# Feed-forward entry of a hybrid decoder block: weight requests, two rows normed in step, block sums by columns between products; norms of the last rows in a batch

## The chip, the cores and the metric

The kernel runs on one core of one Trainium2 chip. The metric is the device time of one execution in microseconds (us); lower is better. Times inside a profile are counted from the start of its span, the stretch from the first to the last instruction.

The engines are named as the profile names them: PE is TensorE (matrix products and transposes; PEld its weight loads), DVE is VectorE, ACT is ScalarE, POOL is GpSimd, and SP is the engine whose queue issues nearly all transfers here. Each works through its own instructions in order and waits for others by semaphores.

## What is computed

One decoder block over 1024 tokens of width 1024, in float32, preceded by 16 meta tokens:

```python
mix = mixer(rms_norm(h, pre_mix_norm), w_in, conv_a_w, conv_b_w, ..., w_out)
h = h + rms_norm(mix, post_mix_norm)
ff = swiglu(rms_norm(h, pre_ffn_norm), w_gate, w_up, w_down)
h = h + rms_norm(ff, post_ffn_norm)

def swiglu(xn, w_gate, w_up, w_down):
    a = jnp.einsum("btd,df->btf", xn, w_gate)
    u = jnp.einsum("btd,df->btf", xn, w_up)
    return jnp.einsum("btf,fd->btd", jax.nn.silu(a) * u, w_down)
```

The feed-forward width is 2816. `mixer` is one input projection, two groups of short convolutions with their gates, and one output projection.

## The kernel before

Every float32 operand of a product is split into a high part (a cast) and a low part (the rest), and `mm3` (lines 94 to 98) makes a product of three matmuls from them: high by high, high by low, low by high.

**Output projection and norms (lines 405 to 468).** The tokens are eight rows of 128, taken in groups (0,1,2), (3,4,5), (6,7). For each group the eight units of w_out are requested, split (cast on ACT, subtraction on POOL, line 88) and multiplied. `leave_psum` squares the result on ACT and multiplies it by the gain (tile jk). `post_mix` requests the row of x, computes an inverse root (`rsqrt_n`, a chain of small DVE instructions, each waiting for the one before), adds to get h and stores it. `ffn_norm` squares h on ACT, makes a second such chain and the normed row hn. `turn` transposes hn on PE and copies it to the four blocks `raw` (two halves of the features by two halves of the rows).

**Feed-forward, up (lines 523 to 677).** Both big products of the feed-forward are made in Strassen's manner: seven block products in place of eight, on sums of blocks. The block sums and splits of the token side (B11, B21, T1, T2, B22, T3, T4) are made once; those of the weight side for each of eleven pairs of feature blocks. A pair has weight units of w_gate (m = 0) and w_up (m = 1), each in two halves i. `order` lists the products (pair j, product n): (0,1), (1,1), (0,2), (1,2), then 6, 5, 7, 3, 4 of pair 0 and of pair 1, then the other pairs. Each has 24 matmuls. The loop at lines 663 to 677 issues a product, then the `leave` of the product before (PSUM to SBUF with the gates), then `a_side(s + LEAD)`, the weight operands of the product two further. In the first two steps it also turns rows 6 and 7; in the second it calls `prepare()` (lines 635 to 644), which makes all that is left of the token side.

**Feed-forward, down (lines 712 to 768).** Seven products of eleven steps each (`down`), with 12 matmuls a step. `run` makes operands two steps ahead (`sides`, `bsum`); the results of a product are left by `leave1` to `leave7` from the list `todo`, up to four a step. The last two steps of a product are issued bank by bank. `finish3` normalises and stores rows 0 to 3 during the last product (n = 4); `leave4` does it for rows 4 to 7 behind it.

**Order.** Up to line 465 a planner orders the instructions by simulated time. From `manual_schedule()` (line 466) to `order_.close()` (line 766) each engine issues its instructions in the order in which they are written; where the first of them fall among the planned ones is left to the planner. Pools give their buffers in turn: `tp` has five tiles of a row (gains, normed rows, weight units), `wp` three of each tag (`ws` for units as they come), `hp` four rows h.

Of the kernel before, what the change touches and what calls it, by code (L numbers as in the profile page):

```python
# [8 lines left out]
F32 = mybir.dt.float32  # L9
F32R = mybir.dt.float32r  # L10
I32 = mybir.dt.int32
AF = mybir.ActivationFunctionType
# [3 lines left out]
P = 128  # L16
# [33 lines left out]
def hybrid_block(ctx: ExitStack, tc: tile.TileContext, xT, x, w_in, w_out, w_gate, w_up, w_down, par, g_post, g_ffn, g_out, out):  # L50
# [377 lines left out]
    def ffn_norm(i, h):  # L428
# [5 lines left out]
        nc.vector.scalar_tensor_tensor(n, h, r2, gB["ffn"], op0=ALU.mult, op1=ALU.mult)  # L434
        return n

    def turn(i, n):
        c = slice((i % 4) * P, (i % 4 + 1) * P)
        for q in range(2):
            pt = aux.tile([P, 512], F32, tag="a", name=f"pt{i}_{q}")  # L440
            for k in range(4):
                nc.tensor.transpose(pt[:, k * P : (k + 1) * P], n[:, (4 * q + k) * P : (4 * q + k + 1) * P], ident)
            p4 = pt.rearrange("p (a b) -> p a b", a=4)
            nc.scalar.copy(raw[q, i // 4][:, :, c], p4)
            if (q, i // 4) == (0, 0):
                nc.vector.tensor_copy(B11[0][:, :, c], p4)
                nc.vector.tensor_tensor(B11[1][:, :, c], p4, B11[0][:, :, c].bitcast(F32), op=ALU.subtract)
# [4 lines left out]
    for grp in ((0, 1, 2), (3, 4, 5), (6, 7)):  # L452
# [16 lines left out]
    ya.close()  # L469
    p2.close()  # L470

    rp = ctx.enter_context(tc.tile_pool(name="rp", bufs=5, side="right", reuse_waits="tile"))
    st = ctx.enter_context(tc.tile_pool(name="st", bufs=13, reuse_waits="tile"))
    psf = None

    def bank(name):
        return (psf or ps2).tile([P, 512], F32, tag="p", name=name)
# [40 lines left out]
    class Pair:  # L523


        def __init__(self, j):
            self.j, self.w, self.pb, self.v = j, [], {}, {}
            for m, src in enumerate((w_gate, w_up)):
                u = []
                for i in range(2):  # L530
                    if (m + i) % 2:
                        t = tp.tile([P, TT], F32, tag="t", name=f"u{j}{m}{i}")[:, :D]
                    else:
                        t = wp.tile([P, D], F32, tag="ws", name=f"u{j}{m}{i}")
                    nc.sync.dma_start(t, src[i * NP + j])
                    u.append(t)
                self.w.append((u[0][:, :512], u[0][:, 512:], u[1][:, :512], u[1][:, 512:]))

        def a_side(self, n, m):
            a11, a12, a21, a22 = self.w[m]  # L540
# [91 lines left out]
    X = {1: B11}  # L632
    r11, r21, r12, r22 = raw[0, 0], raw[1, 0], raw[0, 1], raw[1, 1]

    def prepare():
        halves(sub, r11, r12, r11)
        X[5] = split_big(r11, "T1", (None, None))
        halves(sub, r11, r22, r11)
        X[6] = split_big(r11, "T2", (rp, rp))
        X[3] = split_big(r22, "B22", (rp, rp))  # L640
        halves(sub, r12, r22, r12)
        halves(sub, r21, r21, r11)
        X[7] = split_big(r12, "T3", (None, None))
        X[4] = split_big(r21, "T4", (None, rp))

    pairs = {0: Pair(0), 1: Pair(1)}
    order = [(j, n) for n in (1, 2) for j in range(2)] + [(j, n) for j in range(2) for n in (6, 5, 7, 3, 4)]
    order += [(j, n) for j in range(2, NP) for n in (1, 6, 2, 5, 7, 3, 4)]

    def a_side(s):  # L650
        if s >= len(order):
            return
        j, n = order[s]
        if n == 1 and 2 <= j + 1 < NP and j:
# [6 lines left out]
    for s in range(LEAD):  # L661
        a_side(s)
    for s, (j, n) in enumerate(order):
        if s == 2:
            pa.close()
            psf = ctx.enter_context(tc.tile_pool(name="psf", bufs=8, space=PSUM, reuse_waits="tile"))
        done = pairs[j].product(n, made.pop(s))
        if s < 2:
            turn(6 + s, late[6 + s])
            if s == 0:  # L670
                X[2] = split_big(r21, "B21", (None, None))
            else:
                prepare()
        if last:
            last()
        a_side(s + LEAD)
        last = done

# [21 lines left out]
    def scale(ti, r, parts, q):  # L700

        y, dq = parts[q], slice(q * 512, (q + 1) * 512)
        if q == 1:
# [8 lines left out]
    def down(n, an, bside, banks, begin, leave):  # L712
        for j in range(NP - 2):
            work.append([n, j, an, bside, [(banks[i], i, j, begin and j == 0, False, not begin, None) for i in range(4)]])
        work.append([n, NP - 2, an, bside, []])
        work.append([n, NP - 1, an, bside, [(banks[i], i, j, False, j == NP - 1, not begin, leave) for i in range(4) for j in (NP - 2, NP - 1)]])

    def load(s):
        if s < len(work):
# [23 lines left out]
    def run():  # L743
# [5 lines left out]
        for s, (n, _, _, _, mms) in enumerate(work):  # L749
# [154 lines left out]
```

## Time and profile before

| | us |
|---|---|
| two runs | 1107.70 and 1108.87, median 1108.28 |
| profiled execution | 1107.38 |
| its span | 1105.6 |

| engine | busy us | share of the span | instructions |
|---|---|---|---|
| PE | 1000.7 | 91% | 4643 |
| PEld | 841.7 | 76% | 4643 |
| DVE | 832.1 | 75% | 1176 |
| ACT | 405.1 | 37% | 640 |
| POOL | 362.2 | 33% | 201 |

The page gives for each engine the time that its instructions took. Their starts and lengths are in the timeline, together with the idle time just before an instruction and what ended it: `[22.37 <-ACT U L577]` reads: idle for 22.37 us until the ACT instruction that writes U, of line 577, was done. `x8` means eight instructions of a kind merged into one row. PE's clock is granted by the chip at one of two levels, 1.2 or 2.4 GHz; the profile gives the mean as a share of the higher.

### The profile page before, as it was taken

To read this page: it belongs to the slowest core of one execution; us is meant where nothing else is said; L and a number is where in the kernel's file an instruction comes from. 1 tells how busy PE (TensorE), PEld (TensorE's weight loads), DVE (VectorE), ACT (ScalarE), POOL (GpSimd) and SP (SyncE) were. 2 spreads that over 40 slices of the span, in tenths; PEclk is the share of its full clock that TensorE was granted. 3 is DMA by queue.
4 is the path that set the end of the run, shared out by engine and by line. 5 is a ranking of instruction groups with operands and counts; after the bars stand their busy time and mean duration, and the time that the engine had idled before them with its cause. 6 is when DMAs were issued, how large, how long until landed. Compare 5 with 4: busy or idle time off the path is not lost.

```text
span 1105.6 us, 12729 instructions
## 1 busy us (share of the span) xinstructions
PE 1000.7 (91%) x4643; PEld 841.7 (76%) x4643; DVE 832.1 (75%) x1176; ACT 405.1 (37%) x640; POOL 362.2 (33%) x201
## 2 busy tenths in 40 slices
PE   8999979797988651999999999999999899999974
PEld 8999978796867531888888888888888688887853
DVE  6499999999698849587667767767775565677696
ACT  7345221136445325223232323323231444443442
POOL 3579754254644300034133222413322300010242
PEclk9999989899999865999999999999999999999987
DMA  7111110112365250122430441243027953324232
GB/s 271 58 39 58 39 39 20 58 39 77 114 211 189 76 190 0 49 101 80 143 140 5 142 142 60 83 143 119 24 97 283 390 173 86 105 85 142 88 129 110
DMA packets 44271, 121.56 MB, mean 110 GB/s; under 512 B 4912, under 2 KB 5296, under 8 KB 42800
## 3 DMA queue, kind: packets, MB, share of 16 engines
q1 hardware_dynamic: 43632, 119.10, 31.0%
q10 hardware_dynamic: 576, 1.65, 0.5%
q8 instruction: 36, 0.59, 0.2%
q14 instruction: 27, 0.22, 0.1%
HBM read 92.16 MB, written 28.57 MB: 109 GB/s over the span
## 4 chain that ended last, share of the span: by engine, by line
PE 62%; DVE 26%; issue 5%; ACT 3%; DMA 2%; POOL 1%; POOLq 0%; SPq 0%; DVEq 0%; ACTq 0%
PE x L96 7%; PE x L98 7%; PE x L97 7%; DVE acc L280 6%; DVE z L280 5%; PE y L97 5%; PE y L96 5%; PE y L98 5%; PE qy L97 2%; PE qx L97 2%; PE qy L96 2%; PE qy L98 2%; PE qx L98 2%; PE qx L96 2%; DVE s_pm L118 1%
## 5 line engine op out<-in xcount | busy, mean ns | idle before, releaser
L502 ACT CAST op<-u 128x512 fp32r<-128x512 f32 x132 | 79.1, 618 | 210.3 <-DVE u L491 144.8
L491 DVE TENSOR_TENSOR op<-u,op 128x512 fp32r<-128x512 f32 x132 | 115.3, 899 | 50.9 <-ACT op L502 50.8
L491 DVE TENSOR_TENSOR op_da<-a,op_da 128x512 fp32r<-128x512 f32 x77 | 58.8, 764 | 70.2 <-ACT op_da L502 70.1
L280 DVE SCALAR_TENSOR_TENSOR acc<-g,pr,acc 128x512 f32<-128x512 f32 x146 | 99.9, 748 | 0.0
L494 POOL TENSOR_TENSOR C<-C,C 128x512 f32<-128x512 f32 x11 | 17.4, 1582 | 248.8 <-ACT op L502 129.4
L502 ACT CAST op_da<-a 128x512 fp32r<-128x512 f32 x77 | 47.7, 619 | 100.1 <-issue 49.0
L88 POOL TENSOR_TENSOR wl_o<-ws_o,wh_o 128x1024 fp32r<-128x1024 f32 x24 | 58.4, 2439 | 71.2 <-ACT wh_o L87 71.1
L97 PE MATMUL qx<-op_db,op_da 128*128 128x512 f32 x176 | 70.9, 403 | 9.3 <-DVE op_db L491 9.3
L494 POOL TENSOR_TENSOR U<-U,U 128x512 f32<-128x512 f32 x22 | 31.4, 1426 | 127.9 <-ACT U L606 87.6
L96 PE MATMUL qx<-op_db,op_da 128*128 128x512 f32 x176 | 70.4, 400 | 2.7 <-ACT op_db L502 2.7
L98 PE MATMUL qx<-op_db,op_da 128*128 128x512 f32 x176 | 70.0, 398 | 0.0
L488 DVE TENSOR_TENSOR U<-y,U 128x512 f32<-128x512 f32 x66 | 44.2, 684 | 27.3 <-PE y L98 25.4
L280 DVE SCALAR_TENSOR_TENSOR z<-g,pr,z 128x512 f32<-128x512 f32 x48 | 62.0, 1313 | 0.0
L491 DVE TENSOR_TENSOR op_db<-wd,op_db 128x512 fp32r<-128x512 f32 x77 | 59.2, 769 | 0.0
L96 PE MATMUL x<-B21h,op 128*128 128x512 f32 x88 | 35.5, 403 | 22.4 <-ACT U L577 22.4
L96 PE MATMUL x<-B11h,op 128*128 128x512 f32 x88 | 36.4, 414 | 17.1 <-ACT op L502 17.1
L97 PE MATMUL qy<-op_db,op_da 128*128 128x512 f32 x132 | 51.5, 390 | 0.4 <-DVE op_db L491 0.4
L98 PE MATMUL qy<-op_db,op_da 128*128 128x512 f32 x132 | 51.4, 390 | 0.0
L96 PE MATMUL qy<-op_db,op_da 128*128 128x512 f32 x132 | 51.4, 390 | 0.0
L502 ACT CAST op_db<-wd 128x512 fp32r<-128x512 f32 x77 | 47.5, 617 | 9.1 <-DVE wd L491 9.0
L97 PEld LDWEIGHTS qx<-op_db,op_da 128*128 128x128 f32 x176 | 34.0, 193 | 19.3 <-DVE op_db L491 12.4
L96 PE MATMUL p_in_h<-xh,wh_in_h 128*128 128x342 f32 x96 | 33.1, 344 | 14.9 <-DVE cv L378 14.9
(288 smaller groups left out, 3056.4 us busy)
## 6 DMA issues: line engine op xcount, KB each, us to landing
ws_o<-w_out_u SPq DMA_DIRECT2D x24, 512.0 KB, 3.6
u<-w_gate_u SPq DMA_DIRECT2D x22, 512.0 KB, 6.0
u<-w_up_u SPq DMA_DIRECT2D x22, 512.0 KB, 5.0
wd<-w_down_u SPq DMA_DIRECT2D x11, 1024.0 KB, 11.2
a<-gdS SPq DMA_DIRECT2D x44, 256.0 KB, 2.7
gdS<-GS SPq DMA_DIRECT2D x33, 256.0 KB, 4.8
a<-gdA SPq DMA_DIRECT2D x33, 256.0 KB, 3.6
xs<-xT SPq DMA_DIRECT2D x8, 520.0 KB, 6.9
```

The costliest lines, as they stand in the source:

```text
L88: (eng or nc.gpsimd).tensor_tensor(wl, ws, wh.bitcast(F32), op=ALU.subtract)
L96: nc.tensor.matmul(o, lh, rh, start=start, stop=False, skip_group_check=again)
L97: nc.tensor.matmul(o, lh, rl, start=False, stop=False, skip_group_check=again)
L98: nc.tensor.matmul(o, ll, rh, start=False, stop=stop, skip_group_check=again)
L118: nc.vector.scalar_tensor_tensor(s, t, k, s, op0=ALU.subtract, op1=ALU.mult)
L280: nc.vector.scalar_tensor_tensor(o if j == CB - 1 else p, s, wb(a, j), o if j == HEAD[a] else p, op0=ALU.mult, op1=ALU.add)
L488: (eng or nc.vector).tensor_tensor(o, a, b, op=ALU.add)
L491: (eng or nc.vector).tensor_tensor(o, a, b, op=ALU.subtract)
L494: (eng or nc.vector).tensor_tensor(o, a, b, op=ALU.mult)
L502: nc.scalar.copy(t[:, 0, :], src)
```

## The change

At the entry, the last two rows are no longer normed one after the other. Inside the hand-written order come first: the requests for rows 6 and 7 of x; the requests for the first halves of the weight units of pairs 0 and 1; the operands of the first product; then `norm_two`, which makes one chain for both rows where there were two, twice; then the second halves of pair 0. B21 is split next, its low part on POOL. `prepare()` is gone. What it summed is now summed by columns of one row of tokens each (`tsums`, two rows before the loop, one behind each `turn`), with T2 in a buffer of its own, and the splits of T2, T1, T3, B22 and T4 are each issued behind a product (`extra`).

In the down products two leaves are taken per step in place of four; the last product holds back three steps in place of two and makes its weight sums on POOL; rows 4 to 6 share one chain of the last norm, row 7 has its own and scales both its halves on DVE.

```diff
+    def residual_x(i):
+        h = hp.tile([P, D], F32, tag="h", name=f"h{i}")
+        nc.sync.dma_start(h, x[i * P : (i + 1) * P, :])
+        return h
+
+    def norm_two(grp, left, hs):
+        v = sm.tile([P, 16], F32, tag="s2", name="late1")
+        for q, i in enumerate(grp):
+            nc.vector.tensor_tensor(v[:, q : q + 1], left[i][1][:, 0:1], left[i][1][:, 1:2], op=ALU.add)
+        r = rsqrt_n(v[:, :2], 1.0 / D, RMS_EPS, 2, "pml")
+        v2 = sm.tile([P, 16], F32, tag="s2", name="late2")
+        n = {}
+        for q, i in enumerate(grp):
+            nc.vector.scalar_tensor_tensor(hs[i], left[i][0], r[:, q : q + 1], hs[i], op0=ALU.mult, op1=ALU.add)
+            n[i] = tp.tile([P, TT], F32, tag="t", name=f"hn{i}")[:, :D]
+            nc.scalar.activation(n[i], hs[i], AF.Square, accum_out=v2[:, q : q + 1])
+            nc.sync.dma_start(hd[i], hs[i])
+        r = rsqrt_n(v2[:, :2], 1.0 / D, RMS_EPS, 2, "pfl")
+        for q, i in enumerate(grp):
+            nc.vector.scalar_tensor_tensor(n[i], hs[i], r[:, q : q + 1], gB["ffn"], op0=ALU.mult, op1=ALU.mult)
+        return n
...
-    order_ = ExitStack()
-    order_.enter_context(tc.manual_schedule())
-    late = {i: post_mix(i, *left[i]) for i in grp}
-    late = {i: ffn_norm(i, late[i]) for i in grp}
...
-    def prepare():
-        halves(sub, r11, r12, r11)
-        X[5] = split_big(r11, "T1", (None, None))
-        halves(sub, r11, r22, r11)
-        X[6] = split_big(r11, "T2", (rp, rp))
-        X[3] = split_big(r22, "B22", (rp, rp))
-        halves(sub, r12, r22, r12)
-        halves(sub, r21, r21, r11)
-        X[7] = split_big(r12, "T3", (None, None))
-        X[4] = split_big(r21, "T4", (None, rp))
+    def tsums(i):
+        c = slice(i * P, (i + 1) * P)
+        sub(r11[:, :, c], r12[:, :, c], r11[:, :, c])
+        sub(T2r[:, :, c], r22[:, :, c], r11[:, :, c])
...
+    order_ = ExitStack()
+    order_.enter_context(tc.manual_schedule())
+    late_h = {i: residual_x(i) for i in grp}
+    pairs = {0: Pair(0), 1: Pair(1)}
+    pairs[0].load(0)
+    pairs[1].load(0)
+    a_side(0)
+    late = norm_two(grp, left, late_h)
+    pairs[0].load(1)
...
+    X[2] = pair("B21", (None, None))
+    copy_hi(X[2], r21)
+    for h in range(2):
+        sub(X[2][1][:, 2 * h : 2 * h + 2, :], r21[:, 2 * h : 2 * h + 2, :], X[2][0][:, 2 * h : 2 * h + 2, :].bitcast(F32), nc.gpsimd)
+    T2r = blocks(big("T2r", F32))
+    a_side(1)
+    tsums(0)
+    tsums(1)
...
+    extra = {1: t2, 2: t1, 3: t3, 4: b22, 5: t4}
     for s, (j, n) in enumerate(order):
...
         done = pairs[j].product(n, made.pop(s))
         if s < 2:
-            turn(6 + s, late[6 + s])
-            if s == 0:
-                X[2] = split_big(r21, "B21", (None, None))
-            else:
-                prepare()
+            turn(6 + s, late.pop(6 + s))
+            tsums(2 + s)
         if last:
             last()
+        if s == 2:
+            pairs[1].load(1)
+        if s in extra:
+            extra[s]()
         a_side(s + LEAD)
         last = done
...
-                for f in todo[:4]:
+                for f in todo[:2]:
                     f()
-                todo = todo[4:] + after
+                todo = todo[2:] + after
...
-        mul(t, t, g0, nc.gpsimd if i < 2 else nc.vector)
-        a, b = (ssq[1][dh][:, i : i + 1] for dh in range(2))
-        r = rsqrt_n(a, 1.0 / D, RMS_EPS, 1, f"out{4 + i}", b)
-        for q in range(2):
-            scale(4 + i, r, (t, D22[:, i, :]), q)(nc.sync)
+        mul(t, t, g0, nc.gpsimd)
+        if i < 2:
+            return
+        c = slice(0, 3) if i == 2 else slice(3, 4)
+        a, b = (ssq[1][dh][:, c] for dh in range(2))
+        if i == 2:
+            tot = sm.tile([P, 16], F32, tag="tot", name="tot1")
+            add(tot[:, :3], a, b)
+            a, b = tot[:, :3], None
+        r = rsqrt_n(a, 1.0 / D, RMS_EPS, c.stop - c.start, f"out{4 + i}", b)
+        for k in range(c.start, c.stop):
+            for q in range(2):
+                scale(4 + k, r[:, k - c.start : k - c.start + 1], (E5[:, k, :], D22[:, k, :]), q, k == 3)(nc.sync)
...
-    down(4, "A22", in_place(sub, 2, 2, 0), QX, False, leave4)
+    down(4, "A22", in_place(lambda o, a, b: sub(o, a, b, nc.gpsimd), 2, 2, 0), QX, False, leave4, 3)
```

`t2`, `t1`, `t3`, `b22` and `t4` each make two casts on ACT (`copy_hi`) and two subtractions on DVE (`split_lo`); `t3` and `t4` first make a block sum in two halves on DVE.

## Rows read from the trace of the kernel before

**Rows 1.** Stretches: busy us (x instructions) of PE, PEld, DVE, ACT, POOL; clock; DMA.
```profile
384.20:440.07 55.87, 16.93 (x65) 12.52 (x65) 38.04 (x67) 20.30 (x28) 0.00 (x0) 0.62 0.26 94
1049.20:1089.70 40.50, 33.48 (x133) 26.00 (x131) 34.72 (x61) 17.83 (x38) 15.44 (x10) 0.92 0.30 111
```

**Rows 2.** Timeline of PE: start, us, engine, line, what; idle before and releaser.
```profile
399.33 0.79 PE L96 MATMUL x<-B11h,op 128*128 128x512 f32 x1 [15.83 <-ACT op L502]
...
408.34 1.04 PE L442 MATMUL pt<-ident,hn 128*128 128x128 f32 x8
...
440.07 0.80 PE L96 MATMUL x<-B21h,op 128*128 128x512 f32 x1 [22.37 <-ACT U L577]
...
441.94 0.63 PE L97 MATMUL x<-B21l,op 128*128 128x512 f32 x1
...
452.81 0.40 PE L96 MATMUL y<-T2h,op 128*128 128x512 f32 x1
...
469.56 0.40 PE L96 MATMUL y<-B22h,op 128*128 128x512 f32 x1
```

**Rows 3.** Timeline of all engines, from the last jk to the square of row 7.
```profile
383.58 0.68 DVE L414 TENSOR_TENSOR jk<-po,gB_post 128x512 f32<-128x512 f32 x1
...
387.74 0.42 SPq L419 DMA_DIRECT2D h<-x_tok  x1
...
392.03 1.28 DVE L421 SCALAR_TENSOR_TENSOR h<-jk,s_pm,h 128x1024 f32<-128x1024 f32 x1 [2.49 <-DMA h<-x_tok]
...
393.35 1.06 ACT L432 ACTIVATE hn<-h 128x1024 f32<-128x1024 f32 x1 [4.83 <-DVE h L421]
```

**Rows 4.** Timeline: a POOL subtraction and the DVE instruction that began inside it.
```profile
371.80 2.40 POOL L88 TENSOR_TENSOR wl_o<-ws_o,wh_o 128x1024 fp32r<-128x1024 f32 x1 [1.13 <-ACT wh_o L87]
...
372.24 1.97 DVE L118 SCALAR_TENSOR_TENSOR s_pm<-t_pm,s_pm 128x1 f32<-128x1 f32 x1
```

**Rows 5.** Page, DMA issues: engine, op, count, size of each, median us to landing.
```profile
u<-w_gate_u SPq DMA_DIRECT2D x22, 512.0 KB, 6.0
```

**Rows 6.** Timeline of DVE: first and last of twelve of a chain over four columns.
```profile
1060.39 0.17 DVE L107 TENSOR_SCALAR v_out<-tot 128x4 f32<-128x4 f32 x1
...
1062.58 0.16 DVE L118 SCALAR_TENSOR_TENSOR s_out<-t_out,s_out 128x4 f32<-128x4 f32 x1
```

**Rows 7.** Timeline of ACT and DVE: copies, operands, splits, weight sums, adds from PSUM.
```profile
413.35 1.07 ACT L444 COPY raw<-pt 128x512 f32<-128x512 f32 x2
...
417.67 1.29 DVE L491 TENSOR_TENSOR op<-u,op 128x512 fp32r<-128x512 f32 x2
...
421.20 2.36 DVE L491 TENSOR_TENSOR T1l<-raw,T1h 128x1024 fp32r<-128x1024 f32 x2
...
442.26 0.68 DVE L488 TENSOR_TENSOR S<-u 128x512 f32<-128x512 f32 x1
...
445.69 0.68 DVE L488 TENSOR_TENSOR S<-u 128x512 f32<-128x512 f32 x1
...
459.22 0.68 DVE L491 TENSOR_TENSOR u<-u 128x512 f32<-128x512 f32 x1
...
461.27 0.69 DVE L491 TENSOR_TENSOR u<-u 128x512 f32<-128x512 f32 x1
...
478.35 1.28 DVE L488 TENSOR_TENSOR U<-y,U 128x512 f32<-128x512 f32 x2
```

**Rows 8.** Timeline of PE and POOL in the last product and behind it.
```profile
1053.96 6.38 POOL L494 TENSOR_TENSOR E<-E,gB_out 128x512 f32<-128x512 f32 x4 [25.36 <-ACT jo L692]
...
1065.67 0.79 PE L97 MATMUL qx<-op_db,op_da 128*128 128x512 f32 x1 [3.36 <-DVE op_db L491]
...
1073.20 0.51 PE L97 MATMUL qx<-op_db,op_da 128*128 128x512 f32 x1 [2.04 <-DVE op_db L491]
...
1089.20 0.39 PE L98 MATMUL qx<-op_db,op_da 128*128 128x512 f32 x1
...
1101.21 1.26 POOL L488 TENSOR_TENSOR D<-D,hr 128x512 f32<-128x512 f32 x1 [1.35 <-ACT D L704]
```

More of the change, by code (lines that the diff above doesn't have):

```diff
@@ L464, in hybrid_block @@
                 turn(i, ffn_norm(i, post_mix(i, *left[i])))
[L465 to L479 removed]
+    st = psf = None
     def bank(name):
@@ L526, in __init__, with load @@
         def __init__(self, j):
-            self.j, self.w, self.pb, self.v = j, [], {}, {}
-            for m, src in enumerate((w_gate, w_up)):
[L529 to L532, printed above, removed]
-                    else:
[L534 to L537, printed above, removed]
+            self.j, self.u, self.pb, self.v = j, {}, {}, {}
+            if j >= 2:
+                for i in range(2):
+                    self.load(i)
+        def load(self, i):
+            j = self.j
+            for m, src in enumerate((w_gate, w_up)):
+                if (m + i) % 2 if j >= 2 else i == 1 or (m, j) == (0, 0):
+                    t = tp.tile([P, TT], F32, tag="t", name=f"u{j}{m}{i}")[:, :D]
+                else:
+                    t = wp.tile([P, D], F32, tag="ws", name=f"u{j}{m}{i}")
+                nc.sync.dma_start(t, src[i * NP + j])
+                self.u[m, i] = t
         def a_side(self, n, m):
-            a11, a12, a21, a22 = self.w[m]
+            a11, a12 = self.u[m, 0][:, :512], self.u[m, 0][:, 512:]
+            if n not in (1, 2):
+                a21, a22 = self.u[m, 1][:, :512], self.u[m, 1][:, 512:]
             if n == 1:
@@ L633, in hybrid_block, with split_lo, pair, copy_hi @@
     r11, r21, r12, r22 = raw[0, 0], raw[1, 0], raw[0, 1], raw[1, 1]
-    def prepare():
-        halves(sub, r11, r12, r11)
-        X[5] = split_big(r11, "T1", (None, None))
-        halves(sub, r11, r22, r11)
-        X[6] = split_big(r11, "T2", (rp, rp))
-        X[3] = split_big(r22, "B22", (rp, rp))
-        halves(sub, r12, r22, r12)
-        halves(sub, r21, r21, r11)
-        X[7] = split_big(r12, "T3", (None, None))
-        X[4] = split_big(r21, "T4", (None, rp))
-    pairs = {0: Pair(0), 1: Pair(1)}
+    def tsums(i):
+        c = slice(i * P, (i + 1) * P)
+        sub(r11[:, :, c], r12[:, :, c], r11[:, :, c])
+        sub(T2r[:, :, c], r22[:, :, c], r11[:, :, c])
+    def split_lo(o, src):
+        for h in range(2):
+            s = slice(2 * h, 2 * h + 2)
+            sub(o[1][:, s, :], src[:, s, :], o[0][:, s, :].bitcast(F32))
+    def pair(name, pools):
+        return [blocks(big(f"{name}{j}", pool=p)) for j, p in zip("hl", pools)]
+    def copy_hi(o, src):
+        for h in range(2):
+            s = slice(2 * h, 2 * h + 2)
+            nc.scalar.copy(o[0][:, s, :], src[:, s, :])
     order = [(j, n) for n in (1, 2) for j in range(2)] + [(j, n) for j in range(2) for n in (6, 5, 7, 3, 4)]
     order += [(j, n) for j in range(2, NP) for n in (1, 6, 2, 5, 7, 3, 4)]
+    pairs = {}
     def a_side(s):
@@ L653, in a_side @@
         j, n = order[s]
-        if n == 1 and 2 <= j + 1 < NP and j:
+        if j + 1 < NP and (n == 1 and j >= 2 or n == 6 and j == 1):
             pairs[j + 1] = Pair(j + 1)
@@ L659, in hybrid_block, with t2, t1, t3 @@
     LEAD = 2
-    last = None
-    for s in range(LEAD):
-        a_side(s)
+    order_ = ExitStack()
[7 more added lines that the diff above has]
+    pairs[0].load(1)
+    del late_h, left
+    ya.close()
+    p2.close()
+    rp = ctx.enter_context(tc.tile_pool(name="rp", bufs=5, side="right", reuse_waits="tile"))
+    st = ctx.enter_context(tc.tile_pool(name="st", bufs=13, reuse_waits="tile"))
+    psf = None
+    X[2] = pair("B21", (None, None))
+    copy_hi(X[2], r21)
+    for h in range(2):
+        sub(X[2][1][:, 2 * h : 2 * h + 2, :], r21[:, 2 * h : 2 * h + 2, :], X[2][0][:, 2 * h : 2 * h + 2, :].bitcast(F32), nc.gpsimd)
[3 more added lines that the diff above has]
+    tsums(1)
+    last = None
+    def t2():
+        X[6] = pair("T2", (rp, rp))
+        copy_hi(X[6], T2r)
+        split_lo(X[6], T2r)
+    def t1():
+        X[5] = pair("T1", (None, rp))
+        copy_hi(X[5], r11)
+        split_lo(X[5], r11)
+    def t3():
+        halves(sub, r12, r22, r12)
+        X[7] = pair("T3", (rp, rp))
+        copy_hi(X[7], r12)
+        split_lo(X[7], r12)
+    def b22():
+        X[3] = pair("B22", (None, None))
+        copy_hi(X[3], r22)
+        split_lo(X[3], r22)
+    def t4():
+        halves(sub, r21, r21, T2r)
+        X[4] = pair("T4", (None, None))
+        copy_hi(X[4], r21)
+        split_lo(X[4], r21)
+    extra = {1: t2, 2: t1, 3: t3, 4: b22, 5: t4}
     for s, (j, n) in enumerate(order):
@@ L698, in residual, with scale @@
         nc.sync.dma_start(hr[ti], hd[ti])
-    def scale(ti, r, parts, q):
+    def scale(ti, r, parts, q, both=False):
         y, dq = parts[q], slice(q * 512, (q + 1) * 512)
-        if q == 1:
+        if q == 1 and not both:
             nc.scalar.activation(y, y, AF.Copy, scale=r)
@@ L710, in hybrid_block, with down @@
     work, made, loads = [], {}, {}
-    def down(n, an, bside, banks, begin, leave):
-        for j in range(NP - 2):
+    def down(n, an, bside, banks, begin, leave, held=2):
+        for j in range(NP - held):
             work.append([n, j, an, bside, [(banks[i], i, j, begin and j == 0, False, not begin, None) for i in range(4)]])
-        work.append([n, NP - 2, an, bside, []])
-        work.append([n, NP - 1, an, bside, [(banks[i], i, j, False, j == NP - 1, not begin, leave) for i in range(4) for j in (NP - 2, NP - 1)]])
+        for j in range(NP - held, NP - 1):
+            work.append([n, j, an, bside, []])
+        work.append([n, NP - 1, an, bside, [(banks[i], i, j, False, j == NP - 1, not begin, leave) for i in range(4) for j in range(NP - held, NP)]])
     def load(s):
```

1 line of the change is left out of this document (removed).

## The prediction

> **What bounds the kernel now.** I read the page first, for the slices in which TensorE is idle, then the busy time of stretches, then the timeline engine by engine in the stretches that stood out. Two stretches do. In the first, between the output projection and the feed-forward, TensorE is busy 16.93 of 55.87 us at a mean granted clock of 0.62 while VectorE is busy 38.04 [rows 1]. TensorE waits 15.83 us before its first feed-forward product and 22.37 us before its third [rows 2]; from there to the down projection it is almost never idle. In the second, the last down product and what follows it, TensorE has 7.0 idle us in 40.50 [rows 1], its last matmul starts at 1089.20, and the span ends at 1105.6.
>
> The first wait is a chain of VectorE: both rows end at 384.26 with jk, then come two chains of tiny instructions one after the other, and row 7 waits for its own x, whose request stood behind row 6's store (issued 387.74; h at 392.03) [rows 3]. The first weight request is behind that too. The second wait is `prepare()`: every block sum and split stands ahead of the two PSUM copies that release the banks of product three. So VectorE is the clock of this stage, and TensorE before and behind it has enough to do: products are 5.58 us each (452.81 to 469.56 is three) [rows 2]. I number the products from s0, as `order` does; s7, the first product with B22, starts at 469.56 now. That start is the yardstick.
>
> **The change, step by step.** *Requests.* Both x rows and four weight units are now asked for before the norms. Their buffers come free, the last of them, when GpSimd has split the last w_out unit, 374.20 [rows 4], and a unit lands in 6.0 us in the median [rows 5], so by about 380 to 381; row 7's 2.49 us wait for x falls away. The casts and splits of s0 (two VectorE instructions, 0.6 each) stand ahead of the norms in VectorE's order; up to 378 VectorE has idle time for them, so I take 0, at most 1.2 if they fall later. s0 itself, 5.6 us, can run from the end of the projection, while TensorE has nothing else.
>
> *Norms in step.* From 384.3: two adds 0.4, one chain over two columns 2.3 (the 128x4 chain lasts from 1060.39 to 1062.74 [rows 6]), h6 and h7 2.5: 389.6. ScalarE's square of row 7 takes 1.25 (h7 ends at 393.31 and ACT starts at 393.35 for 1.06, then an accumulator read [rows 3]): 390.9. The second chain would end at 393.2. But `copy_hi` of B21 follows the square on ScalarE, and its two low halves are now on GpSimd from about 392 on, 2.40 us each. The trace shows what that does: a 128x1 instruction of VectorE that began inside a GpSimd subtraction lasted 1.97 us and ended at 374.21, as that one did (374.20) [rows 4]. So the chain is held to about 396.8 and ends at 397.7, 4.5 us late; bounds are 0 and 4.8 (both halves). I take 4.5, since the row is of just this pair.
>
> The Trainium skill, page "SBUF — State Buffer", section "SBUF: two separate sides", has the pair of ports that the two engines share taken by whichever instruction begins first, for its whole length. By that GpSimd might as well be the one that waits, each time a link of the chain has begun first, and the sum below would be 4.5 us better; that is the second case below. "GPSIMD Engine Reference", section "Engine selection", puts elementwise work on VectorE, GpSimd being about 2x slower: 2.40 against 1.18 here, and by it this one move costs VectorE 4.5 us of holding to spare it 2.4.
>
> *To the third product.* hn6 ends at 399.0, hn7 at 400.2 (each as long as h, 1.28 [rows 3]); operands of s1 1.2: 401.4; four column sums 2.6: 404.0. TensorE turns row 6 from 399.0, runs s1 from 400.9 (partly at the low clock after the idle time, some 1.5 us lost) to 408, turns row 7 in 1.0 [rows 2] and reaches 409. ScalarE copies raw twice and then the banks twice, 0.53 each [rows 7]: s2 starts at about 410.2, against 440.07. The first wait is not gone, it is shorter by the x wait, the second chain and the weights; the second is now 1.2 us.
>
> *What is late next.* The sums and splits of `prepare()` are not removed; they move between the products, and there VectorE is slower than TensorE. Per block split 2.36, per pair of operands 1.29, per PSUM add 0.6, operands of (0,6) 3.43 a half and of (0,3) 2.05 a half [rows 7]. From the turn of row 7: its sums end 411.2; T2 and operands of s3 415.9; T1 waits for ScalarE, 418.9; (0,6) 422.4 for the first half, which is when s4 can start (stall 1), 425.8 for the second; product 2's gate, T3 with its sum, operands: s5 starts 431.9 (stall 3.3); B22 and operands 436.6; two adds, T4 with its sum, first half of (0,3): 444.6. s7 starts there, against 469.56: **25.0 us gained**, with 4 us of error either way for these forty-odd terms. From s8 on VectorE's steps are 1.2 to 8 us to TensorE's 5.58 and stay ahead, as in the trace. If VectorE kept up everywhere, s7 would start at 438.1; more than 31.5 cannot come from here.
>
> *Other moves.* T2r, the pools and the stores are in places that nobody waits for: rows' stores go out 2 us after h and are read a half kernel later; the second halves of the weights are issued by 400 and wanted at 419; pair 1's, by 409, wanted at 450. If that cover were gone each would cost its landing, 6 us. The requests queued behind them on SP are pair 2's, wanted in the 470s.
>
> *Down projection.* Two leaves per step instead of four: for product 6 GpSimd's four subtractions no longer come in one block; I take 1.0 of the stall there. In the last product 11 block sums (0.6 us of VectorE each) go to GpSimd at about 1.6, the size of its four in 6.38 [rows 8]. Eleven such hold VectorE for up to 17.6, it saves 6.6; against that, the first sums run early and the four leaves and four scales are spread. The stalls there, 3.36 and 2.04 [rows 8], came from VectorE held by GpSimd. Bounds: +5 (these stalls gone) and -5 (held as computed, less slack). I take 0. Three units held back let banks finish every 2.0 us rather than 1.4.
>
> *The tail.* Now four separate chains, held by GpSimd, end with its add at 1101.21 (1.26) [rows 8]; 3.1 us of store follow. After: rows 4 to 6 share a chain that starts when bank three is left, its end at about +5 from the last matmul; three GpSimd adds to +9.2 hold VectorE; row 7's two scales end at +9.9, then 3.1: 13.0 against 16.0. **3 us**, bounds 1 and 5.
>
> Sum: 25.0 + 1.0 + 0 + 3.0 = 29.0. The profiled execution took 1107.38 (span 1105.6 and 1.8 around it), 0.9 under the median of 1108.28: 1078.4, and with 0.9 **1079**.
>
> **Rivals.** *GpSimd does not hold the chain* (its halves wait, or come after hn7): 4.5 earlier all along VectorE's chain, 1074.5. For it: B21 is first wanted at 410, so GpSimd has time. Against: [rows 4]. *The weight requests are late*: they are put behind row 5's store on SP, or get the buffer of gB_post, free only at 384. Then s0's splits, ahead of the norms on VectorE, wait for a landing at up to 390, everything behind waits 6: 1085. For it: the place of these requests among SP's earlier ones is the scheduler's; against: x of row 6 went out far ahead of its place now. *The last product starves*: GpSimd's queue carries sums, multiplies and adds together, and 2 operands a step held 1.6 each exceed the step of 2.7. Price 5 and a drop of clock, 6: 1085. *The low clock stays*: stalls of 1 to 3 us between s1 and s8 keep TensorE at the lower of its levels; a matmul then lasts 0.63 instead of 0.40 [rows 2], 5.5 us a product. Six such products eat the gain of 29 wherever they bind; all eight, less the stalls that they cover (some 12), make 32: 1111, slower than before. Against: at 440.07 it rose again within 3.5 us of steady matmuls.
>
> The change not doing what it says would be s2 at 440 still; I see no wait that leaves it there.
>
> **Chances.** Forecast 0.47 (own range 1074 to 1086.5), no holding 0.16, late requests 0.15, last product 0.14, low clock 0.05, something unseen and slower 0.03. 2% of 1108.28, about what this measurement can tell, is 22: faster is under 1086.1. From the cases: 0.44 + 0.16 + 0.08 + 0.08 = 0.76 faster; 0.03 + 0.07 + 0.06 + 0.05 = 0.21 same; 0.03 slower. For 8 in 10 the range is 1070 to 1089: most of no holding at the lower end, most of the two losses at the upper.
>
> **What would show it.** Right: s0 before 390; hn6 near 399 with an instruction of its chain lasting about 2 us; s2 near 410; s5 waiting about 3 us for an operand; s7 near 444.6; 13 us behind the last matmul. Wrong: hn6 near 394.5 (no holding); jk followed by a wait for a weight cast (late requests); matmuls of 0.63 behind 412 (clock); over 42 us from first to last matmul of the last product (starved); or a wait in s2 to s8 on a buffer, a bank or ScalarE, which I have at nothing.

## The result and the profile after

The changed kernel takes 1093.83 us (median of two, 1092.7 and 1094.95) against 1108.28. The ratio is 0.987, with a 95% interval of 0.982 to 0.9919: faster by 1.3%. That is 14.5 us, half of the 29 forecast, and outside both ranges that the prediction gave (1074 to 1086.5 and 1070 to 1089). Its profiled execution took 1092.70, with a span of 1090.9 where the span before was 1105.6, so 14.7 us are to be accounted for in the traces.

First the stretches of the kernel after: from the last jk to the first B22 product, then the last three down products, then what follows the last matmul. The columns are those of [rows 1], and the second number is the length.

```profile
384.20:449.38 65.18, 47.48 (x183) 37.74 (x182) 53.97 (x84) 29.07 (x45) 4.65 (x2) 0.82 0.19 66
965.09:997.20 32.11, 30.25 (x134) 24.62 (x132) 24.68 (x34) 12.59 (x23) 5.98 (x4) 1.00 0.38 124
997.20:1030.17 32.97, 30.82 (x133) 24.54 (x132) 22.89 (x26) 14.71 (x31) 12.78 (x8) 1.00 0.29 88
1030.17:1075.22 45.05, 36.45 (x133) 27.41 (x131) 34.95 (x46) 17.91 (x38) 27.02 (x18) 0.89 0.29 99
1075.22:1090.90 15.68, 0.00 (x0) 0.00 (x0) 11.46 (x28) 2.67 (x5) 6.79 (x5) 0.66 0.35 134
```

The three down products, and what follows them, in the kernel before:

```profile
986.21:1018.53 32.32, 30.26 (x133) 24.71 (x132) 24.03 (x34) 12.69 (x23) 5.92 (x4) 1.00 0.36 122
1018.53:1049.20 30.67, 30.25 (x133) 24.71 (x132) 20.47 (x29) 14.77 (x31) 5.96 (x4) 1.00 0.33 95
1049.20:1089.59 40.39, 33.48 (x133) 26.00 (x131) 34.61 (x60) 17.72 (x38) 15.33 (x10) 0.92 0.30 111
1089.59:1105.60 16.01, 0.00 (x1) 0.00 (x0) 11.43 (x40) 3.74 (x8) 5.19 (x5) 0.58 0.35 132
```

Read the lengths against each other. The entry ends 20.2 us earlier (449.38 against 469.56 [rows 2]). The down projection starts 21.0 earlier (842.40 against 863.42); the 0.8 us between are not explained: but for some 2.5 us just before the down projection TensorE is busy all that time, in both kernels. Then 0.2 is gained in product 7, 2.3 lost in product 3, 4.65 lost in the last product, and 0.3 gained behind it: 21.0 + 0.2 - 2.3 - 4.65 + 0.3 = 14.6. In the rest of this text product 7 is `down(7, …)` with S3, product 3 the one behind it with S4, and the last product n = 4 with A22. The last product shows what went wrong in the down projection: 14 instructions fewer on VectorE (46 against 60), the same busy time there (34.95 against 34.61), and 11.7 us more on GpSimd.

The timeline of TensorE in the entry of the kernel after (start, us, engine, line, what; in brackets the idle time before and who ended it):

```profile
399.49 1.94 PE L465 MATMUL pt<-ident,hn 128*128 128x128 f32 x8 [8.58 <-DVE hn L457]
...
410.57 0.51 PE L96 MATMUL x<-B21h,op 128*128 128x512 f32 x1 [1.22 <-ACT U L597]
...
432.53 0.79 PE L96 MATMUL y<-T2h,op 128*128 128x512 f32 x1 [7.90 <-DVE G L508]
433.12 0.63 PE L97 MATMUL y<-T2l,op 128*128 128x512 f32 x1
433.55 0.63 PE L98 MATMUL y<-T2h,op 128*128 128x512 f32 x1
...
449.38 0.39 PE L96 MATMUL y<-B22h,op 128*128 128x512 f32 x1
```

s2 starts at 410.57, where 410.2 was forecast and 440.07 was before [rows 2]. What the entry lacks against the forecast 444.6 is nearly all in one line: in the middle of s4 TensorE waits 7.90 us for `G`, the gate product of (1,2), and comes back at the low clock (0.63 for a matmul until 437.8, with starts 0.43 us apart).

### The profile page after: what moved, and what is told of

The parts are those of the page before. It is cut to its first block, busy times and chain, and to the rows that moved or that the text cites. A ratio compares the mean times of both kernels' runs of the same rounds, so it can differ in the third digit from the quotient of the medians.

```text
span 1090.9 us, 12708 instructions
## 1 busy us (share of the span) xinstructions
PE 1003.6 (92%) x4643; PEld 842.6 (77%) x4643; DVE 832.0 (76%) x1137; ACT 404.4 (37%) x639; POOL 390.2 (36%) x215
## 4 chain that ended last, share of the span: by engine, by line
PE 65%; DVE 24%; issue 4%; ACT 3%; DMA 3%; POOL 1%; SPq 0%; DVEq 0%; ACTq 0%; POOLq 0%
PE x L98 7%; PE x L96 7%; PE x L97 7%; PE y L96 5%; PE y L97 5%; PE y L98 5%; DVE z L280 5%; DVE acc L280 3%; PE qx L97 2%; PE qy L97 2%; PE qy L96 2%; PE qy L98 2%; PE qx L98 2%; PE qx L96 2%; DMA a<-gdA 2%
## 5 line engine op out<-in xcount | busy, mean ns | idle before, releaser
L505 DVE TENSOR_TENSOR op_da<-a,op_da 128x512 fp32r<-128x512 f32 x77 | 62.7, 814 | 72.3 <-ACT op_da L516 72.2
L88 POOL TENSOR_TENSOR wl_o<-ws_o,wh_o 128x1024 fp32r<-128x1024 f32 x24 | 61.2, 2558 | 67.9 <-ACT wh_o L87 67.9
L505 DVE TENSOR_TENSOR op_db<-wd,op_db 128x512 fp32r<-128x512 f32 x77 | 63.4, 823 | 0.0
L505 POOL TENSOR_TENSOR E<-E,E 128x512 f32<-128x512 f32 x4 | 6.0, 1516 | 117.3 <-DVE E L502 117.3
L266 POOL TENSOR_TENSOR z<-z,ct 128x1024 f32<-128x1024 f32 x17 | 43.4, 2553 | 4.9 <-ACT ct L265 4.1
```

Source lines behind the costliest of these rows:

```text
L88: (eng or nc.gpsimd).tensor_tensor(wl, ws, wh.bitcast(F32), op=ALU.subtract)
L266: nc.gpsimd.tensor_tensor(z[a], z[a], t, op=ALU.add)
L505: (eng or nc.vector).tensor_tensor(o, a, b, op=ALU.subtract)
```

## The experiments

All are edits of the changed kernel, and all ratios are to the kernel before, with a 95% interval; it was run again beside them and took 1108.9 to 1109.1. Differences from the changed kernel are differences from its 1093.83, the median of two runs 2.25 us apart, so 1 us of them says little; the stretches of the traces say more. Where the code of the entry is the same, s7 started at 448.30 to 449.63 in six profiles. I first tested the three suspects that the trace named: the gate, GpSimd's B21 and GpSimd's weight sums of the last product.

**The gate of (1,2) earlier.** VectorE, in the kernel after, around the wait:

```profile
425.33 0.68 DVE L508 TENSOR_TENSOR G<-x,G 128x512 f32<-128x512 f32 x1
425.93 2.35 DVE L505 TENSOR_TENSOR raw<-raw,raw 128x1024 f32<-128x1024 f32 x2
428.31 2.36 DVE L505 TENSOR_TENSOR T3l<-raw,T3h 128x1024 fp32r<-128x1024 f32 x2
430.59 1.28 DVE L505 TENSOR_TENSOR op<-S,op 128x512 fp32r<-128x512 f32 x2
431.79 0.68 DVE L508 TENSOR_TENSOR G<-x,G 128x512 f32<-128x512 f32 x1
```

The last of these reads the bank that the second half of (1,2) filled, and the second half of s4 starts 0.06 us after its end (432.47). `G` and this matmul share no buffer of SBUF: so, I concluded, the second half of s4 is given that same bank. The gate of a product is issued one step late (`last`), so behind s3 it stood behind T3, which now lies in that step. The experiment calls it before T3.

```diff
         if s == 2:
             pairs[1].load(1)
+        if s == 3:
+            done()
+            done = None
         if s in extra:
```

> One edit to the changed kernel: the leave of the fourth product, (1,2), is issued directly behind that of the third, ahead of T3 and the operands of (0,5), instead of one step later. Theory (bank): the second half of the fifth product, (0,6), waits 7.9 us because its PSUM bank is the one that (1,2) filled, and the VectorE instruction that empties it stood at 431.8 behind T3 and a pair of operands. Then that half starts at about 426.6 instead of 432.5, the wait falls from 7.9 to about 2 us, VectorE's operands of (0,3) at 445.5 set the first B22 product, which starts at 445.5 to 446 instead of 449.4, and the whole gains about 4 us: 1089.9. Rival (operands): the half waits for its own operands or for TensorE's clock; then it starts near 432 still and the time stays at 1093.8.

1087.75 us (1085.77 to 1088.63), ratio 0.9805 [0.9787, 0.9824]. TensorE:

```profile
427.21 0.50 PE L96 MATMUL y<-T2h,op 128*128 128x512 f32 x1 [2.02 <-DVE G L508]
...
443.79 0.50 PE L96 MATMUL y<-B22h,op 128*128 128x512 f32 x1 [0.32 <-ACT op L516]
```

The wait shrinks from 7.90 to 2.02 and still ends with `G`, the matmuls behind it keep their 0.4, and s7 starts at 443.79, 5.6 earlier and 0.8 ahead of the forecast 444.6. So it was the wait for the bank.

**B21's low half on VectorE.** This tells holding from a delay of another kind.

```diff
-    for h in range(2):
-        sub(X[2][1][:, 2 * h : 2 * h + 2, :], r21[...], X[2][0][...], nc.gpsimd)
     T2r = blocks(big("T2r", F32))
     a_side(1)
+    split_lo(X[2], r21)
```

> One edit to the changed kernel: the low part of B21 is made by VectorE, behind the operands of the second product, not by GpSimd. Theory (holding): the two links of the second chain that lasted 2.35 and 2.26 us last 0.16 again, the chain ends at 393.5 instead of 398, row 6 is turned near 395 instead of 399.5, and with 2.4 us more of its own work VectorE is some 2.2 us earlier at every later step; the third product starts near 408.5 and the total gains about 2 us: 1091.6. Rival (no loss by holding): those two links are long for another reason and stay long; then VectorE is 2.4 us later everywhere, and the time is near 1096.

In the kernel after, GpSimd and the chain of the second norm on VectorE stood so:

```profile
392.30 4.65 POOL L505 TENSOR_TENSOR B21l<-raw,B21h 128x1024 fp32r<-128x1024 f32 x2 [18.41 <-ACT B21h L672]
392.32 2.35 DVE L118 SCALAR_TENSOR_TENSOR s_pfl<-t_pfl,s_pfl 128x2 f32<-128x2 f32 x1
394.71 2.26 DVE L116 TENSOR_TENSOR t_pfl<-s_pfl 128x2 f32<-128x2 f32 x1
```

With the edit:

```profile
392.52 0.16 DVE L118 SCALAR_TENSOR_TENSOR s_pfl<-t_pfl,s_pfl 128x2 f32<-128x2 f32 x1
392.72 0.16 DVE L116 TENSOR_TENSOR t_pfl<-s_pfl 128x2 f32<-128x2 f32 x1
...
397.57 2.35 DVE L505 TENSOR_TENSOR B21l<-raw,B21h 128x1024 fp32r<-128x1024 f32 x2
```

1088.22 us (1087.69 to 1089.62), ratio 0.9814 [0.9797, 0.9831]. The two links of 2.35 and 2.26 are 0.16 each, hn starts at 393.97 (it was 398.06), s2 starts at 405.98 and s7 at 444.60. That is 4.8 gained, not the 2.2 expected: the 2.35 that the split now takes on VectorE fall where VectorE had waited 2.57 for ScalarE's copies of raw. The move to GpSimd spared VectorE 2.35 us in a place where it had time, and cost it 4.3 where it had none. The wait for `G` (7.96) is still there, as it should be.

**A22's sums on VectorE.** Is it GpSimd that starves the last product?

```diff
-    down(4, "A22", in_place(lambda o, a, b: sub(o, a, b, nc.gpsimd), 2, 2, 0), QX, False, leave4, 3)
+    down(4, "A22", in_place(sub, 2, 2, 0), QX, False, leave4, 3)
```

> One edit to the changed kernel: the block sums of the last down product go back from GpSimd to VectorE. Theory (starved by GpSimd's sums): the last product, 45.0 us from its first matmul to the end of its last, comes back to 40 or less, since steps five to nine no longer have two VectorE instructions held 1.1 us each, and the product before it, 33.0, to 30.7; the total gains about 6.5 us: 1087.3. Rival (the leaves by twos do it): the last product stays at 44 to 45 and only the one before gains, 2.3 us: 1091.5.

The last product of the kernel after, on GpSimd, VectorE and TensorE:

```profile
1056.46 5.08 POOL L505 TENSOR_TENSOR wd<-wd 128x512 f32<-128x512 f32 x3
```
```profile
1058.65 1.76 DVE L505 TENSOR_TENSOR op_da<-a,op_da 128x512 fp32r<-128x512 f32 x1
1060.34 1.75 DVE L505 TENSOR_TENSOR op_db<-wd,op_db 128x512 fp32r<-128x512 f32 x1
1062.01 0.68 DVE L505 TENSOR_TENSOR op_da<-a,op_da 128x512 fp32r<-128x512 f32 x1
```
```profile
1055.40 0.50 PE L97 MATMUL qx<-op_db,op_da 128*128 128x512 f32 x1 [2.13 <-DVE op_db L505]
1062.14 0.50 PE L97 MATMUL qx<-op_db,op_da 128*128 128x512 f32 x1 [2.11 <-DVE op_db L505]
```

And the product before it, where the first four sums run at once:

```profile
1009.23 6.83 POOL L505 TENSOR_TENSOR wd<-wd 128x512 f32<-128x512 f32 x4
```
```profile
1009.74 1.77 DVE L505 TENSOR_TENSOR op_da<-a,op_da 128x512 fp32r<-128x512 f32 x1
...
1014.83 1.77 DVE L505 TENSOR_TENSOR op_db<-wd,op_db 128x512 fp32r<-128x512 f32 x1
```

An operand of 0.68 lasts 1.76 as long as GpSimd has a sum under way, and 0.68 again as soon as it has none. With the edit the two products last:

```profile
997.47:1029.08 31.61, 30.22 (x133) 24.69 (x132) 20.49 (x29) 14.66 (x31) 5.98 (x4) 1.00 0.31 92
1029.08:1069.36 40.28, 33.92 (x133) 25.19 (x131) 33.85 (x54) 17.95 (x38) 16.02 (x11) 0.96 0.32 111
```

1089.29 us (1086.85 to 1089.81), ratio 0.9817 [0.9798, 0.9836]. The products fall from 32.97 and 45.05 to 31.61 and 40.28, 6.1 together; the medians show 4.5, where 6.5 was expected. VectorE does eight more instructions in the last product and is busy 1.1 us less. The last product came back as expected; the one before it did not reach 30.7, and the next experiment shows why.

**Four leaves a step again.** The rival for the last product: it starves because leaves come by twos.

```diff
-                for f in todo[:2]:
+                for f in todo[:4]:
                     f()
-                todo = todo[2:] + after
+                todo = todo[4:] + after
```

> One edit to the changed kernel: up to four leaves a step again in the down products. Theory (starved by GpSimd's sums): the last product is not helped by spreading; it stays within 2 us of 45.0, and the total within 2 us of 1093.8; the stall in the product behind S2 stays at about 2 us as in both kernels. Rival (the leaves by twos do it): the last product comes back to about 40.4, and the total is near 1089.

1093.04 us, ratio 0.9856 [0.9838, 0.9875], nothing that can be told from the changed kernel. The last product lasts 45.35 as in the changed kernel 45.05, with two long stalls (3.29 and 5.75) in place of four short ones. The rival falls. All twelve profiles agree: with the sums on GpSimd the last product lasts 45.05 to 45.35 (six), with them on VectorE and leaves by twos 40.24 to 40.32 (four); in the two with the code before it lasts 40.39 and 42.51.

In product 7 the stall, which the expectation calls the one behind S2, is 2.06 here and 1.86 with twos: the forecast gain of 1.0 there is 0.2. In product 3 the twos cost more than that:

```profile
998.04:1030.03 31.99, 30.83 (x134) 24.55 (x132) 22.85 (x26) 14.81 (x31) 12.73 (x8) 1.00 0.31 91
```

| product 3, us | leaves by fours | leaves by twos |
|---|---|---|
| sums on VectorE | 30.67 (before), 30.65 (next experiment) | 31.61 to 31.62 (four profiles) |
| sums on GpSimd | 31.99 (this one) | 32.96 to 32.97 (five profiles) |

So the 2.3 us that the change loses in product 3 are two losses: about 1.35 by GpSimd's sums, about 0.95 by the leaves by twos.

**The entry alone.** The entry of the changed kernel with the down projection and the end of the one before: leaves by fours, the four chains of the next experiment in `leave4`, and A22 as before.

```diff
-    down(4, "A22", in_place(lambda o, a, b: sub(o, a, b, nc.gpsimd), 2, 2, 0), QX, False, leave4, 3)
+    down(4, "A22", in_place(sub, 2, 2, 0), QX, False, leave4)
```

> The changed kernel's entry with the down projection and the end of the kernel before: leaves by four, two steps held back, block sums on VectorE, four chains. Theory (the entry brings about 20 us and the other edits together cost): the first B22 product starts near 449.4, from there on stage by stage the lengths of the kernel before, last product 40.4, 16.0 behind it; the total is 5 us under the changed kernel's: 1088.5. Rival (the edits behind the entry are worth it, the entry brings less than its start times say): no better than 1093.

1088.54 us (1087.37 to 1088.86), ratio 0.9813 [0.9798, 0.9828]. The rest of the change costs some 5 us, then; the entry alone is better than all of it. That the total is the forecast one to 0.1 is luck in part. In the profile s7 started 1.1 earlier than in the changed kernel, product 7 lasted 33.90 (32.32 before), and the last product 42.51, not 40.4, with the code of the kernel before:

```profile
1028.59:1071.10 42.51, 33.10 (x133) 25.90 (x131) 34.72 (x60) 17.73 (x38) 15.37 (x10) 0.92 0.29 105
1045.08 0.50 PE L97 MATMUL qx<-op_db,op_da 128*128 128x512 f32 x1 [3.37 <-DVE op_db L505]
1052.62 0.80 PE L97 MATMUL qx<-op_db,op_da 128*128 128x512 f32 x1 [4.53 <-DVE op_db L505]
```

VectorE does the same as before up to there. In the kernel before TensorE's slow step (0.63 for a matmul) lay between the waits of 3.36 and 2.04 [rows 8] and only shortened the second of them. Here that step ran at 0.39, the second wait was 4.53, and about ten matmuls at the low clock followed it, with no long wait left to hide them.

**The old end.** Only the norms of the last rows as before (four chains).

```diff
-        mul(t, t, g0, nc.gpsimd)
-        if i < 2:
-            return
...
+        mul(t, t, g0, nc.gpsimd if i < 2 else nc.vector)
+        a, b = (ssq[1][dh][:, i : i + 1] for dh in range(2))
+        r = rsqrt_n(a, 1.0 / D, RMS_EPS, 1, f"out{4 + i}", b)
+        for q in range(2):
+            scale(4 + i, r, (t, D22[:, i, :]), q)(nc.sync)
```

> One edit to the changed kernel: the leave of the last product as before, a chain for each of rows 4 to 7 and the multiplies of rows 6 and 7 on VectorE. My prediction had the batch at 3 us: then the stretch from the end of the last matmul to the end of the span grows from 15.7 to 18 or more. Theory (the batch gains nothing, what it saves VectorE is held by GpSimd's multiplies and adds): it stays at 15 to 16.5, and the total at 1093 to 1094.5.

1091.09 us (1090.16 to 1092.9), ratio 0.984 [0.9825, 0.9855]. From the last matmul to the end 14.62 us against 15.68 with the batch, so the batch does not only gain nothing, as the theory had it; it costs 1.1:

```profile
1074.48:1089.10 14.62, 0.00 (x1) 0.00 (x0) 10.06 (x32) 2.95 (x6) 5.50 (x4) 0.67 0.38 143
```

The same four chains took 16.01 in the kernel before and 16.00 in the experiment above, where two steps are held back and not three. Leaves by fours or sums on VectorE leave the 15.7 as it is (15.72 and 15.74), so the third step held back is worth about 1.4 us here; no run tests it by itself. In the trace after, the batch meets GpSimd three times:

```profile
1074.89 1.15 DVE L107 TENSOR_SCALAR v_out<-tot 128x3 f32<-128x3 f32 x1
...
1077.69 1.25 DVE L116 TENSOR_TENSOR t_out<-s_out 128x3 f32<-128x3 f32 x1
...
1083.17 1.21 DVE L118 SCALAR_TENSOR_TENSOR s_out<-t_out,s_out 128x1 f32<-128x1 f32 x1
...
1084.73 0.88 DVE L118 SCALAR_TENSOR_TENSOR s_out<-t_out,s_out 128x1 f32<-128x1 f32 x1
...
1086.37 0.74 DVE L786 SCALAR_TENSOR_TENSOR D<-D,s_out,hr 128x512 f32<-128x512 f32 x1
```
```profile
1074.74 1.27 POOL L508 TENSOR_TENSOR E<-E,gB_out 128x512 f32<-128x512 f32 x1 [0.73 <-ACT jo L771]
...
1077.67 1.26 POOL L508 TENSOR_TENSOR E<-E,gB_out 128x512 f32<-128x512 f32 x1 [1.65 <-ACT jo L771]
...
1080.85 4.74 POOL L502 TENSOR_TENSOR D<-D,hr 128x512 f32<-128x512 f32 x3 [1.92 <-ACT D L783]
```

The first two links are held by the multiplies, and two of row 7's links by the three adds that the batch puts in one block (1080.85 to 1085.59); the last scale begins 11.2 behind the last matmul.

**The multiplies of rows 6 and 7 on VectorE**, with the batch kept.

```diff
-        mul(t, t, g0, nc.gpsimd)
+        mul(t, t, g0, nc.gpsimd if i < 2 else nc.vector)
```

> One edit to the changed kernel: in the last leave the multiplies of rows 6 and 7 are VectorE's again; the batch stays. Theory (holding): the two instructions of the chains that lasted 1.15 and 1.25 us inside those multiplies of GpSimd become short, VectorE takes on 1.2 us of its own in time that it waits for ScalarE, and the stretch behind the last matmul falls from 15.7 to about 14; total 1092. Rival (VectorE is simply full there): 15.7 or more.

1092.85 us, ratio 0.9855 [0.984, 0.9869], the same as with the multiplies on GpSimd within what this can tell; the tail is 15.3, between the theory's 14 and the rival's 15.7. The two links are short, as expected, but what they give is lost at the block of adds: a link of 1.21 and a scale of 1.72 are held there.

**The three together** (gate earlier, B21 and A22 on VectorE).

> Three edits together: the leave of (1,2) early, B21's low part on VectorE, the last block sums on VectorE. Theory: the first two add up, since after both only VectorE's chain is left (5.6 and 4.8 us at the first B22 product: it starts at about 439), the third is behind them (4.8 us in the last product): 1079 to 1080. Rival (with the bank free in time the earlier chain is worth nothing, TensorE binds): the first B22 product stays at 443 to 444 and the total at 1083.

1080.14 us (1076.91 to 1080.63), ratio 0.9731 [0.9712, 0.9749]: 13.7 less than the changed kernel, where the three alone gave 6.1, 5.6 and 4.5. Alone they sum to 16.2, so they are separate causes that nearly add up. In the profiled execution s7 began at 442.08 and not 439. Row 5 was already turned some 2 us later than in the others, I did not find why; then VectorE waited another 0.99 us for the cast of the first weight unit. One of the four runs took 1076.91, the others 1080.06 to 1080.63.

**The three with the old end.**

> The three edits together (leave of (1,2) early, B21's low part and the last block sums on VectorE) and the leave of the last product as before (four chains). Theory: the end alone was worth 1.1 us behind the last matmul (14.6 against 15.7) and has nothing to do with the rest, so the total falls by about 1 from 1080.1: 1079. Rival (the end's gain was chance): 1080 to 1081.

1076.19 us (1075.19 to 1076.86, four runs), ratio 0.9706 [0.9686, 0.9726], the lowest of all: 32 us under the kernel before. That is 4.0 below the three together, where 1 was expected, but the end gives 0.9 of it (14.79 against 15.70). The rest is the entry, which the edit does not touch: s7 starts at 438.64 and not at 442.08, 30.9 earlier than in the kernel before. VectorE in the stage of the entry now:

```profile
412.00:438.00 26.00, 22.49 (x95) 17.19 (x93) 24.12 (x29) 10.82 (x16) 0.00 (x0) 1.00 0.06 21
```

It is busy 24.12 of 26.00 us, and what it waits for there is mostly casts of ScalarE; TensorE is at full clock and waits 2.05 us once more for `G`. So in this stage little is left to gain by another order of VectorE's work.

**The end without GpSimd's adds**, on top of that: rows 4 to 7 scale both halves on VectorE, where D's half went to ScalarE and GpSimd.

```diff
-            scale(4 + i, r, (t, D22[:, i, :]), q)(nc.sync)
+            scale(4 + i, r, (t, D22[:, i, :]), q, True)(nc.sync)
```

> The same, and both halves of rows 4 to 7 are scaled and added by VectorE, none by ScalarE and GpSimd. Theory (holding by GpSimd's adds sets the end): VectorE has four more instructions of 0.67 us, but no link of a chain waits for a GpSimd add any more; the stretch behind the last matmul falls from 14.6 to about 12.6 and the total to 1077. Rival (VectorE is full there and the adds are needed elsewhere): the four instructions come on top, 17, and the total is 1081 to 1082.

1076.70 us (1074.79 to 1077.73), ratio 0.9709 [0.9688, 0.973]. The tail is 13.7 against 14.8, but the total is the same: product 7 took 33.7 in this profile against 32.15, for a reason that is not in the edit (below). Whether it is worth 1 us stays open.

## Why the prediction was wrong, and what of it held

*What held.* The requests for x and the weights were early enough, although those for the weights did go out behind row 5's store (377.21 to 379.08, the landing waited for 1.82 us at the first cast): VectorE lost only the 1.2 that I had as the upper bound, since s0's splits fell among the jk and behind them. The margin is small; in the profile of the three together VectorE waited for that cast. The norms in step, the two links held by B21 (2.35 and 2.26, forecast 4.5 together), hn at 398.06 and s2 at 410.57 came as worked out. The case without holding is excluded by the second experiment, in which hn started 4.1 us earlier once B21's halves were off GpSimd. By the Trainium skill, page "SBUF — State Buffer", section "SBUF: two separate sides", an instruction of VectorE with two inputs in SBUF is kept out for the whole length of a GpSimd one that began first. The trace agrees here: GpSimd began at 392.30, the link at 392.32, and it ended at 394.67, when half of GpSimd's 4.65 us was over. VectorE's chain through s7 came out too: the operand of (0,3) was ready at 445.5, forecast 444.6, with 1.51 us of waiting for TensorE in it.

*The step that failed in the entry: "a wait … on a buffer, a bank or ScalarE, which I have at nothing".* I listed the work of VectorE between the products in its new order and asked when each operand is ready. I did not ask when each bank is left. (1,2)'s gate is issued behind T3, and s4's second half gets (1,2)'s bank. In the sum this stood at 0; it measured 4.8 us at s7 (449.38 against 444.6), and 5.6 by the first experiment. So 20.2 us were gained where 25.0 were forecast. That s7 came within 0.8 us of 444.6 with the bank free is luck in part: I had s5 waiting 3.3 us for operands, and there it waits 0.79 and 0.68, while 2.02 are still the bank's. In the kernel after, s5 waits for nothing, and that sign of being right failed.

*The term of the down projection that was mis-sized: 0 for the last product, with bounds of 5 either way.* It measured -4.65, near the lower bound. I had set the holding of eleven sums (17.6) against slack, and took the middle. The rival "the last product starves", at 0.14 and a price of 5, is the one that took place, shown by the third experiment: 40.28 without the sums on GpSimd. The granted clock fell too, as the rival said: 0.89 in this stretch, 0.92 before, 0.96 in the third experiment. And it lasted 45.05, over the 42 that I had named as the sign.

*The product before it was not costed at all.* I had noted that the first sums run early and counted that on the good side. They run in product 3, 6.83 us in a block, and hold four operands at 1.77 each, which costs about 1.35 us by the third experiment. The other 0.95 of the 2.3 lost there come from the leaves by twos.

*The tail: 3, with a lower bound of 1.* It measured 0.3. I had counted the three adds and not the two multiplies, and had the batch as a saving of instructions. Against the old end behind the same last product VectorE has fewer (28 against 32 in this stretch), but is busy longer (11.46 against 10.06), and the batch costs 1.1; the 0.3 are this loss and the 1.4 of the third step held back. The row-7 scales ended at +11.9 where I had +9.9, and 3.8 us followed where I had 3.1.

*Leaves by twos: 1.0, measured 0.2 in product 7* (1.86 against 2.06) *and a loss of 0.95 in product 3*, which I had not looked at.

*A price in the rival "the low clock stays" was misread.* I took the length of a matmul, 0.63 against 0.40, for the time between two: 5.5 us a product. Ten starts take 4.27 us at the low clock (433.12 to 437.39) and 2.33 otherwise, so the 24 of a product cost 4.7 us more. The rival itself took place only behind the wait of 7.90, for some 14 matmuls.

With the terms as measured: 20.2 and 0.8 up to the start of down, 0.2, -2.3, -4.65, 0.3, in all 14.6. Three of the misses (the last product, part of product 3, the batch) have one root: GpSimd's time was set against VectorE's instructions saved and not against VectorE's instructions held.

## What to carry to other kernels

When work is moved in front of an instruction that empties a bank, find who is given that bank next, and put that time into the sum; a list of operands alone hides it. An elementwise instruction moved from VectorE to GpSimd is not off VectorE where VectorE is busy with instructions of two inputs: set what is held against what is saved. Here a sum of 1.7 us on GpSimd lengthened an operand of 0.68 by 1.08, where it spared VectorE 0.6. A batch of rows saves instructions, but waits for its last member and puts the work behind it in one block; compare busy times, not counts. And where one change bundles several edits, try them apart: here the entry alone was 5 us better than the whole, and what the third held step gained hid part of what the batch lost.

## What the hardware showed that I had not expected

Batched links are easier to hold. In each round the chain of one row has one TENSOR_SCALAR (line 114) where the chain of several has two TENSOR_TENSOR. In the kernel before, that instruction and the first of a chain (line 107) ran inside GpSimd's multiplies without being held:

```profile
1087.08 2.66 POOL L494 TENSOR_TENSOR E<-E,gB_out 128x512 f32<-128x512 f32 x2 [16.95 <-ACT jo L692]
```
```profile
1087.52 0.14 DVE L107 TENSOR_SCALAR v_out<-sp 128x1 f32<-128x1 f32 x1
...
1089.06 0.27 DVE L114 TENSOR_SCALAR t_out<-s_out,v_out 128x1 f32<-128x1 f32 x1
```

Over three columns the TENSOR_TENSOR in the place of line 114 was held (1.25), and so was even the TENSOR_SCALAR 128x3 of line 107 (1.15, ended with GpSimd's multiply).

The clock after a stall of about 2 us is not the same in each execution. In the kernel after, TensorE waits 1.86 us in product 7 and goes on at the 2.4 GHz level, with a granted clock of 1.00 in the 3.75 us that follow. In the last experiment it waits 1.85 in the same place, and the granted clock of the next 3.67 us is 0.54, near the lower level of 1.2 GHz:

```profile
978.25 0.50 PE L97 MATMUL qx<-op_db,op_da 128*128 128x512 f32 x1 [1.86 <-DVE op_db L505]
978.58 0.39 PE L98 MATMUL qx<-op_db,op_da 128*128 128x512 f32 x1
```
```profile
968.73 0.53 PE L97 MATMUL qx<-op_db,op_da 128*128 128x512 f32 x1 [1.85 <-DVE op_db L505]
969.07 0.62 PE L98 MATMUL qx<-op_db,op_da 128*128 128x512 f32 x1
```

With leaves by twos product 7 lasted 32.11 to 32.15 in eight profiles and 33.71 in one, with the same code. With leaves by fours it lasted 32.32 in the kernel before and 33.87 and 33.90 in the experiments, behind the same wait of 2.06 us. So the twos may spare a slow stretch now and then; one in nine against two in three does not show it. A difference of 1.6 us between two profiles is therefore not put down to an edit here. What decides it the runs do not show.
